# A QKV projection with one level of block products: the first four row tiles loaded ahead of w, w by slices, and two small loads from ScalarE

## The chip, the cores and the metric

The kernel runs on one core of a Trainium2 chip. The metric is the device time of one execution in microseconds (us); lower is better. A profiled execution also has a span, from its first to its last instruction, which is a little shorter than the time.

The core has TensorE (PE in the profile, with its weight loads apart as PEld), VectorE (DVE), ScalarE (ACT), GpSimd (POOL) and SyncE (SP), which here only issues DMA transfers. A "q" behind an engine's name means its instruction queue.

## The reference

```python
def reference(x, w_qkv):              # x 16 x 512 x 768, w_qkv 768 x 2304, float32
    qkv = np.matmul(x, w_qkv)
    q = qkv[..., :768]
    k = qkv[..., 768:1536]
    v = qkv[..., 1536:]
    return np.stack([q, k, v], axis=0).astype(np.float32)
```

So it is one product of an 8192 x 768 matrix with a 768 x 2304 matrix, whose result is written as three matrices of 8192 x 768.

## The kernel before

**Tiling.** The 8192 rows of x are taken as 32 pairs (`p`) of two row tiles (`r`) of 128 rows. The 768 values of K are six slices (`j`, KT = 6) of 128, in two halves of three (KH = 3); partition m of slice j holds row 6 m + j of w. The 2304 columns of w are two groups (`q`) of 1024, each two column blocks (`c`) of CB = 512, and 256 remainder columns between them (`w_rem`, REM).

**Steady state.** From row pair 3 on, each pair and column group is computed with seven block products in place of eight (`product`, lines 238 to 252; `do`, lines 260 to 287). The products need sums and differences of the quarters of w (`sum_w`, lines 119 to 127, VectorE: t1 to t4), of the quarters of x (`sums_x`), and a rounded copy of one quarter of w (`b22`). The remainder columns are plain products (`rem`).

**The start.** Nothing of this can begin before w is there, so the first two row pairs (four row tiles) are computed with plain bf16 products, slice by slice as w lands (`block`, lines 436 to 462): block (q=0, c=0), then (q=0, c=1), then the remainder columns of the two pairs. The same two row pairs meet the second column group later, at lines 571 and 585. Row pair 2 is the first with block products (`u`, line 546 on).

In the start x comes as whole rows (`load_row`), is cast to bf16 (`cast_row`: VectorE one half, ScalarE the other), turned by TensorE against an identity into PSUM and copied out again, half by VectorE and half by ScalarE (`turn_row`). A slice of w is cast by `cast_j`. `busy(n)` issues n matmuls of zeros. `load_x_rows(2)` brings row pair 2 in eight parts, which VectorE transposes (`transpose`) and ScalarE rounds (`round_row`).

**Order.** The schedule is written out by hand: each engine runs its instructions in the order of the program text, and each issuing queue issues its transfers in that order. SP's order at the start is: row tiles 0, 1 and 2 (lines 403 to 407), w's slices 0 to 4 of block c=0 (line 408), row tile 3 (line 409), slice 5 (line 410), block c=1 in two halves (line 411), row pair 2 in eight parts (lines 412 and 418), then the second column group's first block (line 419). GpSimd issues w_rem itself (line 417), after a one-column copy, `mark` (line 414), that waits for the first half of block c=1; later in its order comes the rounding of B22 (line 516).

TensorE's order is lines 489 to 520: 8 fillers, row tile 0 turned, 2 fillers, row tile 1 turned, 1 filler, row tile 2 turned, then the products of block 0 with three row tiles per slice. Row tile 3 is turned between slices 4 and 5, and has its six products behind the others (`three`, line 487).

[...]

Of the kernel before, what the change touches and what calls it, by code (L numbers as in the profile page):

```python
# [10 lines left out]
def kernel(  # L11
# [27 lines left out]
    KT = K // P  # L39
# [3 lines left out]
    CB = 512  # L43
# [23 lines left out]
    xb_pool = ctx.enter_context(tc.tile_pool(name="xb", bufs=4))  # L67
    rem_pool = ctx.enter_context(tc.tile_pool(name="rem", bufs=1))
    s_pool = ctx.enter_context(tc.tile_pool(name="s", bufs=2))
    m_pool = ctx.enter_context(tc.tile_pool(name="m", bufs=1))  # L70
    ps_pool = ctx.enter_context(tc.tile_pool(name="ps", bufs=8, space=bass.MemoryType.PSUM))


# [20 lines left out]

    stage = {}

    def load_first(js):
        if (0, 0, 0) not in stage:
            t = tq_pool.tile([P, KT, CB], fp32, name="st0", tag="tq")
            stage[0, 0, 0], stage[0, 1, 0] = t[:, :KH, :], t[:, KH:, :]  # L100
        for j in js:
            load_w(stage[0, j // KH, 0][:, j % KH:j % KH + 1, :], j, 1, Q_OFF[0], CB)

    def load_blocks(q, c):
        if q == 0:
            t = tq_pool.tile([P, KT, CB], fp32, name="st0", tag="tq")
            for j in range(0, KT, KH):
                load_w(t[:, j:j + KH], j, KH, Q_OFF[q] + c * CB, CB)
            stage[q, 0, c], stage[q, 1, c] = t[:, :KH, :], t[:, KH:, :]
        else:  # L110
            for h in range(2):
                if c == 0 and h == 0:
                    t = st_first
                else:
                    t = st_pool.tile([P, KH, CB], fp32, name="st1", tag="st")[:]
                load_w(t, h * KH, KH, Q_OFF[q] + c * CB, CB)
                stage[q, h, c] = t

    def sum_w(q, n):
        t1, t2, t3, t4 = ts[q]  # L120
# [63 lines left out]
    def turn_row(p, r):  # L184
        if r == 0:
            xb[p] = xb_pool.tile([P, KT, 2 * P], bf16, name="xb", tag="xb")
        cols = xc[p][:, r, :].rearrange("m (p j) -> m j p", j=KT)
        ps = ps_pool.tile([P, KT, P], bf16, name="ps")
        for j in range(KT):
            nc.tensor.transpose(ps[:, j, :], cols[:, j, :], eye)  # L190
        ks = (slice(0, KH), slice(KH, KT))
        copy_halves([xb[p][:, n, r * P:(r + 1) * P] for n in ks], [ps[:, n, :] for n in ks])

    def round_x(p):
        xb[p] = xb_pool.tile([P, KT, 2 * P], bf16, name="xb", tag="xb")
# [205 lines left out]
    zero = xb_pool.tile([P, CB], bf16, name="zero", tag="xb")  # L401
    nc.vector.memset(zero[:], 0.0)
    load_row(0, 0)
    nc.scalar.activation(tiny[:], zero[:, :1], ident)
    make_identity(nc, eye)
    load_row(0, 1)
    load_row(1, 0)
    load_first(range(KT - 1))
    load_row(1, 1)
    load_first((KT - 1, ))  # L410
    load_blocks(0, 1)
    load_x_rows(2, (0, ))
    mark = m_pool.tile([P, 1], fp32, name="mark")
    nc.gpsimd.tensor_copy(out=mark[:], in_=stage[0, 0, 1][:, KH - 1, :1])  # L414
    for h in range(2):
        rows = w_qkv.rearrange("(p j) n -> p j n", j=KT)[:, h * KH:(h + 1) * KH]
        nc.gpsimd.dma_start(w_rem[h][:], rows[:, :, R_OFF:R_OFF + REM])  # L417
    load_x_rows(2, range(1, 8))
    load_blocks(1, 0)

    def busy(n):
# [2 lines left out]
        for _ in range(n):  # L424
            nc.tensor.matmul(ps[:], zero[:, :P], zero[:], start=True, stop=True)

    def cast_j(q, c, w, j, eng=act):
        src = stage[q, j // KH, c][:, j % KH, :]
        if eng is act:
            eng.activation(w[:, j, :], src, ident)  # L430
        else:
            eng.tensor_copy(out=w[:, j, :], in_=src)

    quads = {}

    def block(q, c, w, groups, between={}):

        ps = {}
        late = []

        def finish(n):
            p, r = divmod(n, 2)
            u = quads[p, q]
            act.activation(u.o[:, r, c * CB:(c + 1) * CB], ps[n][:], ident)

        for i, (js, tiles) in enumerate(groups):
            for n in tiles:
                p, r = divmod(n, 2)
                if n not in ps:
                    ps[n] = bank()  # L450
                for j in js:
                    nc.tensor.matmul(  # L452
                        ps[n][:], xb[p][:, j, r * P:(r + 1) * P], w[:, j, :],
                        start=(j == 0), stop=(j == KT - 1), skip_group_check=True,
                    )
# [28 lines left out]
        round_x(p)  # L484
        sums_x(p)

    three = [((j, ), range(3)) for j in range(KT)] + [(range(KT), (3, ))]

    busy(8)
    cast_row(0, 0)  # L490
    turn_row(0, 0)
    busy(2)
    cast_row(0, 1)
    cast_row(1, 0)
    turn_row(0, 1)
    busy(1)
    cast_j(0, 0, b1[0], 0, dve)
    turn_row(1, 0)
    for j in range(1, KT - 1):
        cast_j(0, 0, b1[0], j, dve)  # L500
    cast_row(1, 1)
    cast_j(0, 0, b1[0], KT - 1, dve)
    late0 = block(0, 0, b1[0], three, {KT - 2: lambda: turn_row(1, 1)})
    cast_j(0, 1, bt, 0, dve)
    late0[0]()
    late0[1]()
    cast_j(0, 1, bt, 1, act)
    cast_j(0, 1, bt, 2, dve)
    late0[2]()
    late0[3]()  # L510
    sum_w(0, 1)
    cast_j(0, 1, bt, 3, dve)
    cast_j(0, 1, bt, 4, act)
# [123 lines left out]
```

## Time and profile before

| what | value |
|---|---|
| time, three runs | 361.94, 362.08, 362.61 us; median 362.08 |
| time of the profiled execution | 361.55 us |
| its span | 359.7 us |
| TensorE busy | 351.6 us, 98% |
| VectorE, ScalarE, GpSimd busy | 228.3, 186.4 and 178.8 us |
| mean granted TensorE clock | 0.998 |
| DMA moved | 107.70 MB, 299 GB/s in the mean |

The profile is one execution. Busy time of an engine is the time in which it had an instruction; a busy TensorE may still be waiting inside a row of matmuls, since their ends are modelled. The views used here are the page, the chain of work that ended last in order of time, the instructions of one engine in order of time (start, length, engine, line, operation, what is written from what, count, and in brackets the idle time before it and what ended that), and the busy time of the engines in stretches of one microsecond.

| busy from 0 to 24 us, group | count | mean ns |
|---|---|---|
| matmul of zeros (line 425) | 11 | 609 |
| matmul of a block, 128x512 bf16 (line 452) | 47 | 378 |
| matmul of w_rem, 128x256 bf16 (line 304) | 24 | 272 |
| VectorE cast of a slice of w (line 432) | 9 | 424 to 426 |
| ScalarE cast of half a row tile (line 174) | 4 | 521 |
| VectorE cast, or copy from PSUM, of half a row tile (line 173) | 8 | 358 |
| ScalarE evacuation of a block's tile (line 444) | 8 | 601 |
| GpSimd rounding of B22 (line 516) | 1 | 1717 |

### The profile page before, as it was taken

To read this page: it belongs to the slowest core of one execution; us is meant where nothing else is said; L and a number is where in the kernel's file an instruction comes from. 1 tells how busy PE (TensorE), PEld (TensorE's weight loads), DVE (VectorE), ACT (ScalarE), POOL (GpSimd) and SP (SyncE) were. 2 spreads that over 40 slices of the span, in tenths; PEclk is the share of its full clock that TensorE was granted. 3 is DMA by queue.
4 is the path that set the end of the run, shared out by engine and by line. 5 is a ranking of instruction groups with operands and counts; after the bars stand their busy time and mean duration, and the time that the engine had idled before them with its cause. 6 is when DMAs were issued, how large, how long until landed. Compare 5 with 4: busy or idle time off the path is not lost.

```text
span 359.7 us, 5223 instructions
## 1 busy us (share of the span) xinstructions
PE 351.6 (98%) x1744; PEld 250.9 (70%) x1775; DVE 228.3 (63%) x242; ACT 186.4 (52%) x317; POOL 178.8 (50%) x186
## 2 busy tenths in 40 slices
PE   7999999999999999999999999999999999999995
PEld 3465577777777777777777777777777777777763
DVE  3799676657566675566675556676556676556643
ACT  4569744545444545444455444445545445545452
POOL 0401856436665445665444665444665444666420
PEclk9999999999999999999999999999999999999999
DMA  7999999799999999899999999899999899989766
GB/s 270 351 370 358 334 360 337 224 311 337 276 317 304 291 285 281 289 305 310 294 286 281 290 294 328 282 294 274 295 283 323 295 299 271 296 274 326 285 251 246
DMA packets 81611, 107.70 MB, mean 299 GB/s; under 512 B 5041, under 2 KB 61617, under 8 KB 81585
## 3 DMA queue, kind: packets, MB, share of 16 engines
q1 hardware_dynamic: 66464, 96.35, 82.4%
q10 hardware_dynamic: 14320, 10.62, 8.9%
q0 software_dynamic: 800, 0.39, 0.8%
q8 instruction: 14, 0.23, 0.3%
q14 instruction: 13, 0.10, 0.1%
HBM read 32.24 MB, written 75.50 MB: 300 GB/s over the span
## 4 chain that ended last, share of the span: by engine, by line
PE 92%; DMA 5%; issue 1%; ACT 1%; ACTq 0%; POOL 0%; SPq 0%
PE ps L249 78%; PE ps L304 11%; PE ps L452 3%; DMA st<-in_w_qkv_dram 2%; DMA w_rem<-in_w_qkv_dram 2%; DMA xin<-in_x_dram 1%; ACT o L284 0%; ACTq L359 0%; POOL w_rem L417 0%; SPq L170 0%; ACT orem L373 0%; POOL mark L414 0%; ACTq L375 0%; ACTq L373 0%
## 5 line engine op out<-in xcount | busy, mean ns | idle before, releaser
L249 PE MATMUL ps<-t,s 128*128 128x512 f32 x720 | 181.1, 399 | 0.0
L249 PEld LDWEIGHTS ps<-t,s 128*128 128x128 f32 x720 | 135.0, 188 | 30.7
L196 POOL CAST xb<-xf 128x1536 bf16<-128x1536 f32 x28 | 40.9, 1462 | 132.8 <-DVE xf L161 132.8
L281 DVE TENSOR_TENSOR o<-o,ps 128x512 f32<-128x512 f32 x58 | 39.9, 688 | 90.3 <-ACT o L280 90.3
L161 DVE STREAM_TRANSPOSE xf<-xin 128x1536 f32<-128x1536 f32 (+1 forms) x32 | 88.8, 2779 | 1.6 <-DMA xin<-in_x_dram 1.6
L249 PE MATMUL ps<-b,xb 128*128 128x512 bf16 x331 | 85.1, 380 | 1.5
L249 PEld LDWEIGHTS <-xb 128*128 128x128 bf16 x360 | 32.8, 98 | 37.3 <-issue 7.6
L274 ACT ACTIVATE o<-ps 128x512 f32<-128x512 f32 x60 | 35.9, 598 | 43.7 <-PE ps L249 40.9
L280 ACT ACTIVATE o<-ps 128x512 f32<-128x512 f32 x58 | 34.7, 599 | 44.3 <-PE ps L249 44.3
L287 DVE TENSOR_TENSOR o<-o,ps 128x512 f32<-128x512 f32 x60 | 41.3, 688 | 21.4 <-PE ps L249 20.2
L249 PE MATMUL ps<-b,s 128*128 128x512 f32 x180 | 50.4, 389 | 0.0
L284 ACT ACTIVATE o<-ps 128x512 f32<-128x512 f32 x60 | 35.9, 598 | 24.5 <-PE ps L249 21.6
L258 ACT ACTIVATE o<-ps 128x512 f32<-128x512 f32 x60 | 35.9, 598 | 24.4 <-DVE o L287 20.6
L304 PE MATMUL ps<-w_rem,xb 128*128 128x256 bf16 x384 | 47.5, 273 | 0.3 <-DMA w_rem<-in_w_qkv_dram 0.3
L304 PEld LDWEIGHTS <-xb 128*128 128x128 bf16 x384 | 37.2, 98 | 12.0 <-issue 1.6
L271 DVE TENSOR_TENSOR o<-o,ps 128x512 f32<-128x512 f32 x60 | 37.9, 674 | 2.2 <-ACT o L258 1.6
L249 PEld LDWEIGHTS ps<-b,s 128*128 128x128 f32 x180 | 33.8, 188 | 7.1
L216 POOL TENSOR_TENSOR s<-xf 128x384 fp32r<-128x384 f32 x29 | 30.9, 1065 | 0.0
L217 POOL TENSOR_TENSOR s<-s,xf 128x384 fp32r<-128x384 f32 x29 | 29.5, 1018 | 2.3
L218 POOL TENSOR_TENSOR s<-xf 128x384 fp32r<-128x384 f32 x29 | 29.5, 1017 | 0.0
L220 POOL TENSOR_TENSOR s<-xf,s 128x384 fp32r<-128x384 f32 x29 | 29.5, 1016 | 0.0
L318 ACT ACTIVATE orem<-ps 128x512 f32<-128x512 f32 x31 | 18.5, 596 | 20.1 <-PE ps L304 20.1
(44 smaller groups left out, 119.9 us busy)
## 6 DMA issues: line engine op xcount, KB each, us to landing
out_dram<-o SPq DMA_DIRECT2D x62, 768.0 KB, 5.3
out_dram<-o SPq DMA_DIRECT2D x65, 256.0 KB, 4.2
xin<-in_x_dram SPq DMA_DIRECT2D x62, 192.0 KB, 6.9
xin<-in_x_dram ACTq DMA_DIRECT2D x50, 192.0 KB, 4.6
out_dram<-orem SPq DMA_DIRECT2D x31, 256.0 KB, 5.9
st<-in_w_qkv_dram SPq DMA_DIRECT2D x5, 768.0 KB, 8.7
xin<-in_x_dram SPq DMA_DIRECT2D x4, 384.0 KB, 4.4
st<-in_w_qkv_dram SPq DMA_DIRECT2D x6, 256.0 KB, 5.8
```

The lines of the kernel that those rows point to most:

```text
L161: nc.vector.transpose(turned[:, g:g + n], rows[:, g:g + n])
L196: nc.gpsimd.tensor_copy(out=xb[p][:], in_=xf[p][:])
L216: 1: lambda g: g.tensor_tensor(s[:, 1], a21, a22, op=add),
L249: nc.tensor.matmul(ps[:], lhs[j], rhs[j], start=(start and j == 0), stop=(j == KH - 1), skip_group_check=True,)
L258: nc.scalar.activation(u.o[:, 0, :CB], u.x[:], ident)
L271: nc.vector.tensor_tensor(c11, c11, u.z[:], op=add)
L274: nc.scalar.activation(c12, u.x[:], ident)
L280: nc.scalar.activation(c22, u.x[:], ident)
L281: nc.vector.tensor_tensor(c22, c22, u.y[:], op=add)
L284: nc.scalar.activation(c21, u.x[:], ident)
L287: nc.vector.tensor_tensor(c12, c12, u.y[:], op=add)
L304: nc.tensor.matmul(ps, xb[p][:, j, r * P:(r + 1) * P], w_rem[j // KH][:, j % KH, :], start=(j == 0), stop=(j == KT - 1), skip_group_check= ...
```

## The change

SP's order becomes: row tiles 0, 1, 2 and 3; w's block c=0 by slices, the first slice in two halves of 256 columns; block c=1 by slices, six transfers in place of two; row pair 2 in eight parts with nothing between; then the second column group as before. ScalarE issues two loads first of all, of 32 values (128 bytes) in each of 128 rows: of w's first slice, and of row tile 2 of x. Their destination, `touch`, is read by nothing.

GpSimd's mark now waits for the first slice of block c=1; a second mark, behind w_rem and ahead of B22's rounding, waits for the first half of row pair 2.

`turn_row` puts its two halves into two PSUM tiles and hands back the copies out of PSUM, which the caller issues later. All four row tiles are turned ahead of the first product. Block 0 runs four row tiles per slice; its first slice runs for three of them in two column halves. The first three slices of block c=1 are all cast by VectorE, where ScalarE did the second, and the four evacuations of block 0 are issued behind them.

```diff
-    m_pool = ctx.enter_context(tc.tile_pool(name="m", bufs=1))
+    m_pool = ctx.enter_context(tc.tile_pool(name="m", bufs=2))
...
+    def load_slices(c, cuts):
+        t = tq_pool.tile([P, KT, CB], fp32, name="st0", tag="tq")
+        stage[0, 0, c], stage[0, 1, c] = t[:, :KH, :], t[:, KH:, :]
+        for j, nj, lo, hi in cuts:
+            load_w(t[:, j:j + nj, lo:hi], j, nj, Q_OFF[0] + c * CB + lo, hi - lo)
...
         cols = xc[p][:, r, :].rearrange("m (p j) -> m j p", j=KT)
-        ps = ps_pool.tile([P, KT, P], bf16, name="ps")
+        ks = (slice(0, KH), slice(KH, KT))
+        ps = [ps_pool.tile([P, KH, P], bf16, name="ps") for _ in ks]
         for j in range(KT):
-            nc.tensor.transpose(ps[:, j, :], cols[:, j, :], eye)
-        ks = (slice(0, KH), slice(KH, KT))
-        copy_halves([xb[p][:, n, r * P:(r + 1) * P] for n in ks], [ps[:, n, :] for n in ks])
+            nc.tensor.transpose(ps[j // KH][:, j % KH, :], cols[:, j, :], eye)
+        return lambda: copy_halves(
+            [xb[p][:, n, r * P:(r + 1) * P] for n in ks], [t[:] for t in ps]
+        )
...
     load_row(0, 0)
+    touch = m_pool.tile([P, 2, G], fp32, name="touch")
+    nc.scalar.dma_start(touch[:, 0], w_qkv.rearrange("(p j) n -> p j n", j=KT)[:, 0, :G])
+    nc.scalar.dma_start(touch[:, 1], x_flat[2 * P:3 * P, :G])
     nc.scalar.activation(tiny[:], zero[:, :1], ident)
     make_identity(nc, eye)
     load_row(0, 1)
     load_row(1, 0)
-    load_first(range(KT - 1))
     load_row(1, 1)
-    load_first((KT - 1, ))
-    load_blocks(0, 1)
-    load_x_rows(2, (0, ))
-    mark = m_pool.tile([P, 1], fp32, name="mark")
-    nc.gpsimd.tensor_copy(out=mark[:], in_=stage[0, 0, 1][:, KH - 1, :1])
+    half = CB // 2
+    load_slices(0, [(0, 1, 0, half), (0, 1, half, CB)] + [(j, 1, 0, CB) for j in range(1, KT)])
+    load_slices(1, [(j, 1, 0, CB) for j in range(KT)])
+    load_x_rows(2)
+
+    def hold(src):
+        mark = m_pool.tile([P, 1], fp32, name="mark")
+        nc.gpsimd.tensor_copy(out=mark[:], in_=src)
+
+    hold(stage[0, 0, 1][:, 0, :1])
     for h in range(2):
         rows = w_qkv.rearrange("(p j) n -> p j n", j=KT)[:, h * KH:(h + 1) * KH]
         nc.gpsimd.dma_start(w_rem[h][:], rows[:, :, R_OFF:R_OFF + REM])
-    load_x_rows(2, range(1, 8))
+    hold(xin[2][:, 0, :1])
     load_blocks(1, 0)
...
-    three = [((j, ), range(3)) for j in range(KT)] + [(range(KT), (3, ))]
+    lo, hi = slice(0, half), slice(half, CB)
+    first = [((0, ), range(3), lo), ((0, ), range(3), hi), ((0, ), (3, ))]
+    first += [((j, ), range(4)) for j in range(1, KT)]
 
     busy(8)
     cast_row(0, 0)
-    turn_row(0, 0)
+    turned = [turn_row(0, 0)]
     busy(2)
+    turned[0]()
     cast_row(0, 1)
+    turned.append(turn_row(0, 1))
+    busy(2)
     cast_row(1, 0)
-    turn_row(0, 1)
+    turned[1]()
+    turned.append(turn_row(1, 0))
     busy(1)
-    cast_j(0, 0, b1[0], 0, dve)
-    turn_row(1, 0)
-    for j in range(1, KT - 1):
+    cast_row(1, 1)
+    turned[2]()
+    cast_j(0, 0, b1[0], 0, dve, lo)
+    turned.append(turn_row(1, 1))
+    cast_j(0, 0, b1[0], 0, dve, hi)
+    turned[3]()
+    for j in range(1, KT):
         cast_j(0, 0, b1[0], j, dve)
-    cast_row(1, 1)
-    cast_j(0, 0, b1[0], KT - 1, dve)
-    late0 = block(0, 0, b1[0], three, {KT - 2: lambda: turn_row(1, 1)})
-    cast_j(0, 1, bt, 0, dve)
-    late0[0]()
-    late0[1]()
-    cast_j(0, 1, bt, 1, act)
-    cast_j(0, 1, bt, 2, dve)
-    late0[2]()
-    late0[3]()
+    late0 = block(0, 0, b1[0], first)
+    for j in range(KH):
+        cast_j(0, 1, bt, j, dve)
+    for f in late0:
+        f()
     sum_w(0, 1)
     cast_j(0, 1, bt, 3, dve)
```

`block` and `cast_j` take a range of columns for this. In `block` only the first matmul into a row tile's PSUM bank has the start flag; the second column half and the later slices come without it.

More of the change, by code (lines that the diff above doesn't have):

```diff
@@ L95 @@
     stage = {}
[L97 to L102, printed above, removed]
-    def load_blocks(q, c):
[L105 to L117, printed above, removed]
+    def load_slices(c, cuts):
[3 more added lines that the diff above has]
+            load_w(t[:, j:j + nj, lo:hi], j, nj, Q_OFF[0] + c * CB + lo, hi - lo)
+    def load_blocks(q, c):
+        for h in range(2):
+            if c == 0 and h == 0:
+                t = st_first
+            else:
+                t = st_pool.tile([P, KH, CB], fp32, name="st1", tag="st")[:]
+            load_w(t, h * KH, KH, Q_OFF[q] + c * CB, CB)
+            stage[q, h, c] = t
     def sum_w(q, n):
@@ L425, in busy, with cast_j @@
             nc.tensor.matmul(ps[:], zero[:, :P], zero[:], start=True, stop=True)
-    def cast_j(q, c, w, j, eng=act):
-        src = stage[q, j // KH, c][:, j % KH, :]
+    def cast_j(q, c, w, j, eng=act, n=slice(0, CB)):
+        src = stage[q, j // KH, c][:, j % KH, n]
         if eng is act:
-            eng.activation(w[:, j, :], src, ident)
+            eng.activation(w[:, j, n], src, ident)
         else:
-            eng.tensor_copy(out=w[:, j, :], in_=src)
+            eng.tensor_copy(out=w[:, j, n], in_=src)
     quads = {}
@@ L444, in finish @@
             act.activation(u.o[:, r, c * CB:(c + 1) * CB], ps[n][:], ident)
-        for i, (js, tiles) in enumerate(groups):
+        for i, (js, tiles, *cols) in enumerate(groups):
+            cols = cols[0] if cols else slice(0, CB)
             for n in tiles:
                 p, r = divmod(n, 2)
-                if n not in ps:
+                fresh = n not in ps
+                if fresh:
                     ps[n] = bank()
@@ L452, in block @@
                     nc.tensor.matmul(
-                        ps[n][:], xb[p][:, j, r * P:(r + 1) * P], w[:, j, :],
-                        start=(j == 0), stop=(j == KT - 1), skip_group_check=True,
+                        ps[n][:, cols], xb[p][:, j, r * P:(r + 1) * P], w[:, j, cols],
+                        start=(fresh and j == 0), stop=(j == KT - 1), skip_group_check=True,
                     )
```

## The prediction

> **Order of reading.** First the page: TensorE is busy 98% of the span, and from 22.9 us on the chain of waits lists nothing but matmuls up to the last evacuations at 352 us. So a change to the start is worth just what it takes off, or adds to, the time before that dense stretch, if nothing else in the kernel becomes late. Then the chain in order of time, which says what bounds the start:
>
> ```profile
> 1.65 5.21 DMA xin<-in_x_dram
> 6.88 6.73 DMA st<-in_w_qkv_dram
> 13.67 0.44 POOL mark L414
> 14.11 0.85 POOL w_rem L417
> 14.96 5.42 DMA w_rem<-in_w_qkv_dram
> 20.43 2.45 PE ps L304 x21
> ```
>
> Columns: start, length, what. Until 20.43 us the end is set by loads: rows of x, the first 512 columns of w, the next 512 (c=1), and the remainder columns w_rem, which GpSimd asks for only after the first half of c=1 has landed and its mark is made. Next, TensorE in order of time:
>
> ```profile
> 8.13 3.41 PE L452 MATMUL ps<-b,xb 128*128 128x512 bf16 x15
> 11.67 0.54 PE L190 MATMUL ps<-eye,xc 128*128 128x128 bf16 x6
> 12.20 2.10 PE L452 MATMUL ps<-b,xb 128*128 128x512 bf16 x8
> 14.13 5.65 PE L452 MATMUL ps<-both,xb 128*128 128x512 bf16 x24
> 19.62 0.49 PE L304 MATMUL ps<-w_rem,xb 128*128 128x256 bf16 x3
> 20.43 2.45 PE L304 MATMUL ps<-w_rem,xb 128*128 128x256 bf16 x21 [0.31 <-DMA w_rem<-in_w_qkv_dram]
> ```
>
> The 15 matmuls start every (3.41 - 0.38) / 14 = 0.216 us, those of w_rem every 0.109 us (2.45 less one of 0.27, over 20). Block 0 (24 matmuls; one record is missing) needs 24 x 0.216 = 5.18 us and takes 14.13 - 8.13 = 6.00: 0.82 is the break 11.37 to 12.20, where the fourth row tile is cast, turned and copied. Block 1 needs 5.18 and takes 19.62 - 14.13 = 5.49: 0.31 is lost to the cast of its last slices. Then 3 x 0.109 bring us to 19.95, and TensorE stands still 0.48 us until 20.43. So 1.61 us are there to be won, beside the first matmul's place at 8.13. The landings are read off VectorE, where it waited:
>
> ```profile
> 6.89 0.36 DVE L173 CAST xc<-xin 128x384 bf16<-128x384 f32 x1 [0.80 <-DMA xin<-in_x_dram]
> ...
> 9.47 0.43 DVE L432 CAST b<-st 128x512 bf16<-128x512 f32 x1 [0.22 <-DMA st<-in_w_qkv_dram]
> 10.17 0.43 DVE L432 CAST b<-st 128x512 bf16<-128x512 f32 x1 [0.27 <-DMA st<-in_w_qkv_dram]
> 11.09 0.36 DVE L173 CAST xc<-xin 128x384 bf16<-128x384 f32 x1 [0.50 <-DMA xin<-in_x_dram]
> 11.72 0.43 DVE L432 CAST b<-st 128x512 bf16<-128x512 f32 x1 [0.26 <-DMA st<-in_w_qkv_dram]
> ...
> 16.61 3.02 DVE L127 TENSOR_TENSOR t<-st,t 128x1536 fp32r<-128x1536 f32 x1
> ```
>
> Third row tile 6.89, fourth 11.09, w's sixth slice 11.72: a row tile (384 KB) costs 11.09 - 10.17 = 0.92 us of the queue, a slice (256 KB) about 0.65. Last the stretches of one us (PE, PEld, DVE, ACT, POOL, clock, DMA share, GB/s):
>
> ```profile
> 4.00:5.00 1.00, 1.00 (x6) 0.55 (x5) 0.19 (x1) 0.35 (x1) 0.00 (x0) 1.00 0.88 344
> 5.00:6.00 1.00, 1.00 (x6) 0.37 (x4) 0.54 (x2) 0.15 (x1) 0.00 (x0) 1.00 0.95 282
> 6.00:7.00 1.00, 0.47 (x4) 0.20 (x4) 0.20 (x2) 0.86 (x3) 0.00 (x0) 1.00 1.01 370
> ...
> 11.00:12.00 1.00, 0.87 (x9) 0.38 (x8) 0.64 (x2) 0.52 (x1) 0.00 (x0) 1.00 1.05 410
> ```
>
> The DMA engines are full from 6 us on, but move 344, 282 and 370 GB/s from 4 to 7 us against 410 later: 66 + 128 + 40 = 234 KB are missing, 0.57 us at 410. That is the stretch of the third row tile and of w's first slice, the two places that the new 128-byte loads read ahead.
>
> **Row tile 4 ahead of w.** SP issues its load before w's, so it lands at 6.89 + 0.92 = 7.81 and all of w's slices up to the sixth keep their sum (11.72). TensorE now turns it before the first product: ScalarE's cast 0.52, 0.06 to TensorE, six transposes and a start behind them 0.40, so 7.81 + 0.02 + 0.98 = 8.81. Beside it VectorE casts its half (0.36), copies row tile 3 (0.36) and casts the low half of w's first slice (half of 0.43), each overlapping the next by some 0.08: about 8.80 too. The half slice itself lands at 7.81 + 0.32 = 8.13, earlier than VectorE gets to it. First matmul 8.81 instead of 8.13: **+0.68**. The break goes: **-0.82**. The three further fillers (busy) and the earlier copies lie before 8.13 on idle engines; two PSUM tiles per turn let ScalarE copy beside VectorE, where it waited 3.1 us in all before.
>
> **Column halves and four tiles per slice.** Three matmuls of 512 columns become six of 256: 6 x 0.109 against 3 x 0.216, nothing. Four tiles use 0.86 us per slice and a slice lands every 0.65, so from the second slice (9.10, cast by 9.55, due at 8.81 + 0.86 = 9.67) loads stay ahead. Block 0 ends at 8.81 + 5.18 = 13.99.
>
> **c=1 by slices.** Six issues for two, and two for one in w's first slice: five more at some 0.55 (five took 2.78) are 2.8 us of SP's sequencer. Hidden: SP spends 8.21 to 16.57 on the eight issues for row pair 2, waiting for earlier landings; without that cover row pair 2 would start up to 2.8 us late. The slices land from about 12.4 in steps of 0.65, so VectorE's three casts (now all there) are done by 14.1, sum 1 (1.75) by 15.8, the fourth slice's cast by 16.25; TensorE wants it at 13.99 + 12 x 0.216 = 16.58. ScalarE has four evacuations (2.2) and two casts (1.15) from 13.7: 17.0, wanted at 17.01. So block 1 loses its stall, by a hair: **-0.31**, end 19.17. Bounds: -0.31 and 0.
>
> **w_rem earlier.** The mark now waits for one slice (12.4), not half of c=1 (13.64): GpSimd issues 1.24 us earlier. Low end: w_rem lands at 20.43 - 1.24 = 19.19, wanted at 19.17 + 0.33 = 19.50, the wait is gone, -0.48. High end: the DMA engines are full anyway, w_rem shares them with row pair 2 and lands at 20.43 as before; then everything won so far is waited away here. From 17 to 18 us 314 of 391 packets were w_rem's: once its descriptors are there it goes ahead of row pair 2. So nearer the low end; I take a landing at 19.60, a wait of 0.10: **-0.38**.
> [...]
>
> **Rounding B22 later** takes GpSimd's 1.7 us off VectorE's sum 2, which took 3.02 beside it against 1.75 alone. No time on the path: TensorE needs B22 only after 27.4 us, and it is made by about 20.5. It now runs beside the transposes of row pair 2, where no row shows the pair: 0 to 1.27 us. The cover: row pair 2's first half is wanted at about 22.0, and transposed (1.54) and rounded (0.85) by 20.5, or 21.8. The second mark queues only B22 behind it.
>
> **The two small loads.** ScalarE issues them before its table load (0.73 to 2.0) and is wanted at 3.83; at 0.43 each they hide. On the engines 256 packets: upper bound from w_rem's 512-byte packets, 117.2% of 16 engine-us for 314, 60 ns, so 256 x 60 / 16 = 0.96 us; lower bound a gain of 0.57, if the missing 234 KB come back. Both shift all loads, hence everything above. A quarter of 512 bytes is nearer the low price; I take 0.3 spent, 0.3 won: **0**.
> [...]
>
> **Sum.** 0.68 - 0.82 - 0.31 - 0.38 = -0.83 us. Later work keeps it: row pair 2's sums had about 1.2 us to spare before TensorE's use at 25.24, the next slices' casts about 1.0. The profiled execution took 361.55 (span 359.7, 1.85 around it), the runs 362.08 in the median, 0.53 more; -0.83 on the median is 361.25, I say **361.2**.
>
> **Rivals.**
> 1. *The wait moves to w_rem* (0.22). For it: full DMA engines from 6 to 20 us, and the same bytes. Against: the 314 packets. TensorE is held to about 20.43 and the gain is 0 to 0.2: 361.9 to 362.1. The case that the small loads warm nothing and cost 0.6 to 0.8 ends here too.
> 2. *The small loads pay in full* (0.20). For it: 282 GB/s exactly where w's first slice begins. Then loads come 0.57 earlier: -1.4, 360.7.
> 3. *The small loads sit ahead of the first row tile on the same engines* (0.13): they queue with it from 1.7 us, it lands at up to 4.8, and the chain of rows keeps the 0.96. From 0.83 on the change loses. At the full price with w_rem held as well: first matmul 9.77, block 1 ends 20.13, w_rem 20.43 + 0.96 = 21.39: +0.96, 363.0. Against: early engines are not full (267 GB/s from 2 to 3 us), so part hides.
>
> The forecast itself has 0.45. Its own range is 360.9 to 361.6. What can be told from no change is 0.2%, 0.72 us, so faster means below 361.36: two thirds of the forecast (0.30), rival 2 (0.20), a little of rival 1: 0.52. Same: the rest of the forecast and most of rival 1: 0.34. Slower: rival 3 and a remainder: 0.14. The range 360.3 to 362.6 leaves out the far ends of rivals 2 and 3.
>
> **What would show it.** First product near 8.8 with no break up to 19.2; row tile 4's cast near 7.8; the mark near 12.4; the w_rem wait at 0.1 or gone; sum 2 at 1.75; GB/s from 4 to 7 us near 400 for rival 2. I am wrong if the first row tile's cast moves from 3.83 by more than 0.5, if the w_rem wait is 0.5 or more, or if a new wait stands between 22 and 46 us.

## The result, and the profile after

| what | before | after |
|---|---|---|
| time, median of 22 runs each | 362.06 us (361.37 to 363.53) | 361.15 us (360.58 to 362.73) |
| ratio after / before | | 0.9979, 95% interval 0.9970 to 0.9988 |
| time of the profiled execution | 361.55 us | 360.69 us |
| its span | 359.7 us | 358.9 us |
| mean granted TensorE clock | 0.998 | 1.0 |

The change takes 0.91 us off in the median, about 0.2%. The prediction said 361.2 with a range of 360.3 to 362.6. Its sum was -0.83; in the two profiled executions it is made up of other terms than were forecast, as the views show.

First the start of the chain of waits of the changed kernel (start, length, what):

```profile
2.12 5.36 DMA xin<-in_x_dram
7.50 4.54 DMA st<-in_w_qkv_dram
13.38 6.39 DMA w_rem<-in_w_qkv_dram
19.82 2.45 PE ps L299 x21
```

The same four loads bound the start as before. TensorE is released for good at 19.82 instead of 20.43, 0.61 earlier, and w_rem's transfer now takes 6.39 us from issue to landing, where it took 5.42. TensorE in order of time:

```profile
8.08 0.54 PE L184 MATMUL ps<-eye,xc 128*128 128x128 bf16 x6 [0.34 <-ACT xc L167]
8.45 5.38 PE L456 MATMUL ps<-b,xb 128*128 128x256 bf16 x27
13.67 5.34 PE L456 MATMUL ps<-both,xb 128*128 128x512 bf16 x24
18.85 0.49 PE L299 MATMUL ps<-w_rem,xb 128*128 128x256 bf16 x3
19.82 2.45 PE L299 MATMUL ps<-w_rem,xb 128*128 128x256 bf16 x21 [0.48 <-DMA w_rem<-in_w_qkv_dram]
```

The break at 11.67 is gone: block 0 takes 13.67 - 8.45 = 5.22 us, block 1 takes 18.85 - 13.67 = 5.18. Both are dense. The three matmuls of w_rem end at 18.85 + 3 x 0.109 = 19.18, and TensorE stands still until 19.82: **0.64 us**, more than the 0.48 of before. From there the two executions run in step, up to the last row of w_rem's matmuls (the first line is from before, the second from after):

```profile
354.86 0.83 PE L304 MATMUL ps<-w_rem,xb 128*128 128x256 bf16 x6
354.27 0.83 PE L299 MATMUL ps<-w_rem,xb 128*128 128x256 bf16 x6
```

That is 0.59 earlier, but the time of the profiled execution is 0.86 less. The time less the start of this row was 6.69 us and is 6.42: 0.27 us lie behind the last matmuls. They aren't in the transfers of the last outputs, which are 0.6 earlier too (the DMA engines fall idle between 357.4 and 357.6, where it was between 358.0 and 358.2). No term of the prediction is about this end.

VectorE in order of time, for the landings and what lies next to the rounding of B22:

```profile
4.11 0.36 DVE L166 CAST xc<-xin 128x384 bf16<-128x384 f32 x1 [2.98 <-DMA xin<-in_x_dram]
...
6.35 0.36 DVE L166 CAST xc<-xin 128x384 bf16<-128x384 f32 x1 [0.63 <-DMA xin<-in_x_dram]
...
7.50 0.36 DVE L166 CAST xc<-xin 128x384 bf16<-128x384 f32 x1 [0.52 <-DMA xin<-in_x_dram]
...
15.74 1.75 DVE L120 TENSOR_TENSOR t<-st,t 128x1536 fp32r<-128x1536 f32 x1
17.58 1.60 DVE L154 STREAM_TRANSPOSE xf<-xin 128x768 f32<-128x768 f32 x1
20.85 1.57 DVE L154 STREAM_TRANSPOSE xf<-xin 128x768 f32<-128x768 f32 x1 [1.67 <-DMA xin<-in_x_dram]
```

The first row tile lands 0.28 later than before (4.11 against 3.83), the third 0.54 earlier (6.35 against 6.89), the fourth at 7.50. Sum 2 is back at 1.75 us. GpSimd:

```profile
12.09 0.44 POOL L414 COPY mark<-st 128x1 f32<-128x1 f32 x1 [10.78 <-DMA st<-in_w_qkv_dram]
12.47 1.70 POOL L419 DMA_DIRECT2D w_rem<-in_w_qkv_dram  x2
...
17.74 1.47 POOL L525 CAST b<-st 128x1536 fp32r<-128x1536 f32 x1
```

The mark is made 1.58 us earlier than before (13.67), yet w_rem lands only 0.61 earlier. B22's rounding now lies beside the transpose at 17.58, which takes 1.60; the other transpose, with no work of GpSimd beside it, takes 1.57. The stretches of one us (PE, PEld, DVE, ACT, POOL, clock, DMA share, GB/s):

```profile
4.00:5.00 1.00, 0.76 (x7) 0.32 (x6) 0.36 (x1) 0.52 (x1) 0.00 (x0) 1.00 0.99 363
5.00:6.00 1.00, 0.66 (x6) 0.16 (x4) 0.62 (x2) 0.74 (x2) 0.00 (x0) 1.00 1.00 350
6.00:7.00 1.00, 0.78 (x8) 0.56 (x9) 0.64 (x2) 0.81 (x3) 0.00 (x0) 1.00 0.99 360
```

The stretch that moved 344, 282 and 370 GB/s now moves 363, 350 and 360: 77 KB of the 234 KB that were missing are back.

### The profile page after: what moved, and what is told of

The parts are those of the page before. It is cut to its first block, busy times and chain, and to the rows that moved or that the text cites. A ratio compares the mean times of both kernels' runs of the same rounds, so it can differ in the third digit from the quotient of the medians.

```text
span 358.9 us, 5279 instructions
## 1 busy us (share of the span) xinstructions
PE 352.3 (98%) x1780; PEld 251.0 (70%) x1780; DVE 227.4 (63%) x244; ACT 185.7 (52%) x316; POOL 178.6 (50%) x187
## 4 chain that ended last, share of the span: by engine, by line
PE 92%; DMA 5%; ACT 1%; ACTq 0%; POOL 0%; SPq 0%; issue 0%
PE ps L244 78%; PE ps L299 11%; PE ps L456 3%; DMA w_rem<-in_w_qkv_dram 2%; DMA xin<-in_x_dram 1%; DMA st<-in_w_qkv_dram 1%; SPq L163 0%; ACT o L279 0%; ACTq L354 0%; POOL w_rem L419 0%; ACT orem L368 0%; POOL mark L414 0%; ACTq L370 0%; ACTq L368 0%
## 5 line engine op out<-in xcount | busy, mean ns | idle before, releaser
L244 PE MATMUL ps<-b,xb 128*128 128x512 bf16 x360 | 87.7, 380 | 0.0
L213 POOL TENSOR_TENSOR s<-xf 128x384 fp32r<-128x384 f32 x29 | 29.4, 1013 | 0.0
L211 POOL TENSOR_TENSOR s<-xf 128x384 fp32r<-128x384 f32 x29 | 29.3, 1011 | 0.0
```

The source lines that it names most:

```text
L244: nc.tensor.matmul(ps[:], lhs[j], rhs[j], start=(start and j == 0), stop=(j == KH - 1), skip_group_check=True,)
```

## The experiments

All kernels compute the whole result. Each time is a median beside runs of the kernel before on the same chip: 362.18 us (29 runs) for e1 to e4, 362.15 (29) for e5, e6, e8 and e10, 361.89 (35) for e7, e11, e12 and e13. The ratios come with the comparison and need not be the quotients of these medians. A profile is one execution and carries the spread of one: e13 is the changed kernel once more, and its profiled execution takes 361.47, its median 360.94.

Times of the start in all profiles. "Row 4" is VectorE's cast of the fourth row tile (its landing), "mark" GpSimd's first mark, "go" the start of w_rem's second half on TensorE, "end" the start of the last row of w_rem's matmuls, and "time - end" the time of the profiled execution less that. (In e6 VectorE had other work ahead of row 4's cast, so 9.20 is no landing there.)

| kernel | first row | row 4 | first product | mark - row 4 | go - row 4 | end | time - end | ratio to before, 95% |
|---|---|---|---|---|---|---|---|---|
| before | 3.83 | 11.09 | 8.13 | | | 354.86 | 6.69 | |
| after | 4.11 | 7.50 | 8.45 | 4.59 | 12.32 | 354.27 | 6.42 | 0.9979, 0.9970 to 0.9988 |
| e13 after again | 4.01 | 7.88 | 8.84 | 4.60 | 12.73 | 355.06 | 6.41 | 0.9978, 0.9968 to 0.9988 |
| e1 no small loads | 3.72 | 8.21 | 9.16 | 4.59 | 13.01 | 355.65 | 6.55 | 0.9982, 0.9970 to 0.9994 |
| e2 small loads alone | 4.12 | 10.86 | 8.11 | | | 354.77 | 6.79 | 0.9991, 0.9976 to 1.0005 |
| e3 w_rem late | 4.10 | 8.91 | 9.86 | 6.16 | 12.84 | 356.20 | 6.43 | 0.9983, 0.9968 to 0.9998 |
| e4 w_rem early | 4.09 | 8.05 | 9.01 | 3.30 | 12.41 | 354.91 | 6.42 | 0.9961, 0.9946 to 0.9976 |
| e5 B22 early | 4.13 | 7.84 | 8.79 | 4.59 | 12.59 | 354.87 | 6.42 | 0.9977, 0.9964 to 0.9990 |
| e7 c=1 in halves | 4.03 | 7.75 | 8.70 | 5.88 | 12.46 | 354.66 | 7.03 | 1.0014, 0.9998 to 1.0030 |
| e8 row pair 2 held | 3.86 | 7.56 | 8.61 | 4.61 | no wait | 354.25 | 6.46 | 0.9974, 0.9959 to 0.9990 |
| e10 w_rem from SP | 3.80 | 7.90 | 8.85 | | no wait | 355.45 | 6.53 | 0.9990, 0.9975 to 1.0004 |
| e11 row 4 turned ahead | 3.91 | 7.89 | 9.00 | | no wait | 355.43 | 6.99 | 1.0016, 1.0003 to 1.0029 |
| e12 order | 3.86 | 8.28 | 9.23 | | no wait | 354.74 | 6.42 | 0.9974, 0.9964 to 0.9985 |
| e6 row 4 alone | 3.62 | 9.20 | 11.59 | | no wait | 358.47 | 6.69 | 1.0093, 1.0059 to 1.0126 |

The column "time - end" parts the kernels in two: 6.41 to 6.55 where block c=1 comes by slices, 6.69 to 7.03 where it comes in halves (before, e2, e6, e7, e11). This is not only the spread of single profiles. The part of it that lies outside the span is on record for every run: 1.74 to 1.86 us in the 12 of e13 (median 1.77), 1.77 to 2.07 in the 35 of the kernel before beside them (median 1.97). So 0.2 us of e13's gain lie outside the span. The profiles show as much again inside it, behind the last matmuls: from the start of their last row to the end of the span it is 4.8 us before, 4.6 after and in e13. The cause of both is open.

**The small loads (e1, e2).** e1 is the changed kernel without them, e2 the kernel before with nothing but them (and its second buffer).

```diff
-    touch = m_pool.tile([P, 2, G], fp32, name="touch")
-    nc.scalar.dma_start(touch[:, 0], w_qkv.rearrange("(p j) n -> p j n", j=KT)[:, 0, :G])
-    nc.scalar.dma_start(touch[:, 1], x_flat[2 * P:3 * P, :G])
```

> The changed kernel without ScalarE's two 128-byte loads. Theory A, the loads cost and win about as much (0.21 us of the engines by 256 packets of 13 ns, against the cold start of w's first slice): first product within 0.2 us of the 8.45 of the changed kernel, last row of w_rem within 0.2 of 354.27, time as the changed kernel's 361.2. Rival B, they pay in full: the loads of the third and fourth row tile land 0.3 to 0.6 us later (the fourth at 7.8 to 8.1 in place of 7.50), first product 8.8 to 9.0, GB/s from 5 to 6 us back near 280, time 361.5 to 361.8. Rival C, they are pure cost: the first row tile lands at 3.8 in place of 4.11 and all is 0.2 to 0.3 earlier.

> The kernel before with ScalarE's two small loads alone. Theory A: third row tile's cast within 0.3 us of 6.89, end within 0.2 of before, 362.1. Rival B, they pay in full: third row tile 6.3, w's slices 0.5 earlier, and since w_rem follows its mark the end comes 0.5 earlier, 361.6. Rival C: first row tile 4.1 and everything 0.2 to 0.3 later, 362.3.

Measured: 361.72 without them (12 runs), 361.84 with them alone (12 runs). Over all profiles of the study the first row tile is cast at 3.62 to 3.91 in the four without them (mean 3.77) and at 3.80 to 4.13 in the ten with them (mean 4.01): they cost 0.24 us there. The third row tile is cast at 6.36 to 7.77 without (mean 7.07) and at 6.1 to 7.98 with them (mean 6.72): 0.35 earlier, with a spread five times as large, so a gain there isn't shown. What they take of the engines is small. The queue of ScalarE's loads in the changed kernel from 3 to 4 us (packets, MB, share of the 16 engines):

```profile
q10 hardware_dynamic: 121, 0.01, 9.4%
```

By this 9.4% of 16 engine-us over 121 packets, an estimate is 12 ns each. The times lean to a gain, 0.34 us in the medians of e2 (361.84 against 362.18) and, by the ratios of after and e1 (0.9979 and 0.9982), 0.1; neither interval parts it from nothing. No harm from them can be seen; whether they gain anything stays open.

**w_rem's mark moved both ways (e3, e4).** e3 waits with the mark for the third slice of c=1, about where it stood before; e4 for the fifth slice of c=0.

```diff
-    hold(stage[0, 0, 1][:, 0, :1])
+    hold(stage[0, 0, 1][:, KH - 1, :1])      # e3
+    hold(stage[0, 1, 0][:, 1, :1])           # e4
```

> The changed kernel with the mark on the third slice of block c=1, as before, in place of the first: GpSimd asks for w_rem 1.3 us later. Theory A, w_rem goes as soon as it is asked for: it lands near 21.1 in place of 19.82, TensorE waits 1.9 us in place of 0.65, last row of w_rem 355.5 in place of 354.27, time 362.4, that is slower than the kernel before. Rival B, the full engines set the landing whatever the mark does: landing 19.8 to 20.4, time 361.2 to 361.8.

> The changed kernel with the mark on the fifth slice of block c=0: GpSimd asks for w_rem 1.2 us earlier. Theory A: w_rem lands near 18.6, the wait of 0.65 us is gone, last row of w_rem 353.7 in place of 354.27, time 360.6, unless block c=1 is late (its fourth to sixth slices share the engines with w_rem then and may land up to 1 us later, a stall of up to 0.5). Rival B, full engines: w_rem lands at 19.5 or later and the time stays 361.1.

Measured: 361.48 (12 runs) and 361.16 (6 runs). The late mark was to cost all that was won, and did not. The table says why: counted from the fourth row tile, the mark moves over 2.86 us (3.30 to 6.16), and w_rem's go over 0.43 (12.41 to 12.84), while two profiles of one and the same kernel differ by 0.41 (12.32 and 12.73). When w_rem lands hardly depends on when it is asked for: its second half takes 5.34 us from issue to landing in e3, 6.39 and 6.79 in the two profiles of the changed kernel, 7.76 in e4. A small gain from asking early isn't excluded: e4 has the lowest ratio of all, 0.9961, from six runs, though its block 1 takes 5.39 us, and VectorE's sum 2 waits 0.52 us for the last slices of c=1, as it would if they now share the engines with w_rem. In the changed kernel GpSimd asks, from 12.47 on, while the engines are full of c=1 (a DMA share of 1.04 to 1.05 from 12 to 15 us), and then w_rem shares them with row pair 2. The DMA queues from 17 to 18 us (packets, MB, share of the 16 engines), first two lines of before, then two of the changed kernel:

```profile
q0 software_dynamic: 314, 0.16, 117.2%
q1 hardware_dynamic: 77, 0.05, 21.5%
...
q0 software_dynamic: 280, 0.14, 102.2%
q1 hardware_dynamic: 127, 0.09, 32.7%
```

The queue of GpSimd's w_rem moved 280 packets beside 127 of SP's row pair 2. Before, it was 314 beside 77. I had taken the 314 as a sign that w_rem goes ahead of the rest; in the changed kernel's stretch it goes about two packets to one. So neither queue was simply first in that stretch; what decides between them, no run here shows.

**Row pair 2 out of w_rem's way (e8).** If the sharing sets w_rem, then holding back row pair 2 must free it. e8 keeps SP from issuing the second half of row pair 2 until c=1's last slice is there (a small GpSimd copy into `xin` comes ahead of it).

```diff
-    load_x_rows(2)
+    load_x_rows(2, range(4))
...
+    nc.gpsimd.tensor_copy(out=xin[2][:, 4:, 0], in_=stage[0, 1, 1][:, KH - 1, :4])
+    load_x_rows(2, range(4, 8))
```

> The changed kernel with row pair 2's second half (parts 5 to 8) held back on SP until block c=1 has wholly landed, so that fewer of its packets share the engines with w_rem. Theory C, w_rem's landing is set by what shares the DMA engines with it: w_rem lands 0.3 to 0.6 us earlier than in the changed kernel by the same landing of row tile 3, TensorE's wait falls from 0.65 to 0.1 to 0.4, time 360.7 to 361.0. Rival: w_rem's landing does not move, since its own 768 packets set it, time 361.1 to 361.3; or row pair 2 comes late and TensorE waits behind w_rem's rows.

Measured: 361.32 (12 runs), 0.9974, no other than the changed kernel. TensorE and VectorE in its profile, each in order of time:

```profile
18.98 2.78 PE L299 MATMUL ps<-w_rem,xb 128*128 128x256 bf16 x24
21.59 1.46 PE L244 MATMUL ps<-b,xb 128*128 128x512 bf16 x5
22.89 1.55 PE L299 MATMUL ps<-w_rem,xb 128*128 128x256 bf16 x12
24.58 0.73 PE L244 MATMUL ps<-t,s 128*128 128x512 f32 x2
```

```profile
21.10 1.58 DVE L154 STREAM_TRANSPOSE xf<-xin 128x768 f32<-128x768 f32 x1 [1.85 <-DMA xin<-in_x_dram]
```

All 24 matmuls of w_rem run in one piece: the wait is gone, and w_rem's halves take 5.2 and 5.6 us from issue to landing, where it was 5.9 and 6.4 (asked for from 12.55 on, the second is in use at 19.31, 18.98 + 3 x 0.109, where it was 19.82). So the sharing was its cause. But row pair 2's second half is there at 21.10 instead of 20.85, and behind its transpose, ScalarE's rounding (22.72) and an evacuation (23.94) TensorE now stops for 0.4 us ahead of 24.58. The wait has moved to the next load in the same row.

**Other ways past it (e10, e12).** e10 loads w_rem on SP's queue as float32, ahead of row pair 2, and GpSimd casts it (the first mark is left out). e12 is e8 with the hold one slice earlier, and with row pair 2's first product and its evacuation ahead of ScalarE's second rounding.

```diff
+    for h in range(2):                                                     # e10
+        load_w(wst[:, h * KH:(h + 1) * KH], h * KH, KH, R_OFF, REM)
...
-        nc.gpsimd.dma_start(w_rem[h][:], rows[:, :, R_OFF:R_OFF + REM])
+        nc.gpsimd.tensor_copy(out=w_rem[h][:], in_=wst[:, h * KH:(h + 1) * KH])
```

```diff
+    nc.gpsimd.tensor_copy(out=xin[2][:, 4:, 0], in_=stage[0, 1, 1][:, KH - 2, :4])     # e12
+    load_x_rows(2, range(4, 8))
...
+    u = quad(2, 0)
+    do(u, 1)
```

> The changed kernel with w_rem loaded by SP as float32, in its order behind block c=1 and ahead of row pair 2, and cast by GpSimd (two casts of 0.73 us). Theory C: nothing shares the engines with it, it lands at about 16.5 and 17.5, is cast by 18.3, and TensorE's wait is gone: last row of w_rem 353.6 to 353.7 in place of 354.27, time 360.4 to 360.7. Row pair 2 lands at about 20.7 as now. Rival: the wait is not DMA sharing, and a wait of like size comes up next (row pair 2's transposes and copies behind w_rem's rows), time 361.0 or more.

> An attempt to beat the changed kernel: row pair 2's second half held back until the fifth slice of c=1 has landed (so w_rem shares the engines with less), and TensorE's first product of row pair 2 with its evacuation put ahead of ScalarE's second rounding of row pair 2. Theory C: the wait for w_rem is at most 0.3 and the next wait (0.4 in the run with the half held to the sixth slice) at most 0.2; last w_rem row less first product 345.2 to 345.5 in place of 345.82, time 360.7 to 361.0. Rival: the DMA engines' total up to row pair 2 sets it, and what w_rem gains is waited away at row pair 2: difference 345.6 or more, time as the changed kernel.

Measured: e10 361.88 (12 runs), a miss: w_rem's wait is gone, but row pair 2 is transposed at 19.77 and 22.32, and TensorE waits 0.28 and 0.39 for it. e12 361.10 (12 runs) beside 360.94 (12 runs) for e13, the changed kernel, on the same chip: no difference that can be told.

> The changed kernel once more, to be compared on this chip with the three others of this call and for a second profile of its start: time 360.9 to 361.4; first product 0.98 us behind row tile 3's landing, whatever the landing is in this execution; a wait for w_rem of 0.5 to 1.0.

Measured: 360.94 (12 runs). TensorE in its profile, in order of time:

```profile
8.84 5.38 PE L456 MATMUL ps<-b,xb 128*128 128x256 bf16 x26
14.05 5.34 PE L456 MATMUL ps<-both,xb 128*128 128x512 bf16 x24
19.23 0.49 PE L299 MATMUL ps<-w_rem,xb 128*128 128x256 bf16 x3
20.61 2.45 PE L299 MATMUL ps<-w_rem,xb 128*128 128x256 bf16 x21 [0.89 <-DMA w_rem<-in_w_qkv_dram]
```

The first product is 0.96 behind the fourth row tile, and the wait for w_rem is 20.61 - (19.23 + 0.33) = 1.05, just above what was expected. Here TensorE is released 0.18 later than in the profile of before, though the median is 0.95 less than before's. The two don't contradict each other: e13's profiled execution (361.47) is among the slowest of its 12 runs, those of before (361.55) and after (360.69) are each faster than all but one of the 22 runs. Two profiles show how the parts of one start hang together. They don't show what each part is worth of the 0.9 us in the medians.

Three kernels (e8, e10, e12) rid TensorE of the wait for w_rem and none is faster than the changed kernel by more than can be told. I take what is left of the start to be the sum of the bytes up to row pair 2, through engines that are full (a DMA share of 0.99 or more in every us from 3 to 20 in the changed kernel); no run moves fewer bytes, so that is argued, not shown.

**The fourth row tile alone (e6).** The kernel before with its SP order changed and the fourth tile turned ahead, but with the old `turn_row`, whose copies follow at once and share one PSUM tile.

```diff
-    load_first(range(KT - 1))
     load_row(1, 1)
-    load_first((KT - 1, ))
+    load_first(range(KT))
...
-    three = [((j, ), range(3)) for j in range(KT)] + [(range(KT), (3, ))]
+    three = [((j, ), range(4)) for j in range(KT)]
...
+    turn_row(1, 1)
+    for j in range(KT):
+        cast_j(0, 0, b1[0], j, dve)
+    late0 = block(0, 0, b1[0], three)
```

> The kernel before with one part of the change: row tile 3 loaded ahead of w and turned ahead of the first product, four row tiles per slice; w's first slice whole, the turn with one PSUM tile, c=1 in halves, mark and B22 as before, no small loads. Theory A (first product 0.98 us behind the landing of row tile 3, plus 0.3 to 0.6 for the turn's two copies in a row and the whole slice): first product 9.2 to 9.6, no break, block 0 ends at 14.4 to 14.8 in place of 14.13, and TensorE waits for w_rem until 20.4 as before: time 362.1, no change, since w_rem's landing is what the start waits for. Rival: the break taken away is the gain, time 361.4 or less.

Measured: 366.11 (6 runs, 362.46 to 366.94), the largest miss of the study. ScalarE, then TensorE, in order of time, and the stretches of one us:

```profile
8.43 0.49 ACT L174 ACTIVATE xb<-ps 128x384 bf16<-128x384 bf16 x1
9.31 0.49 ACT L174 ACTIVATE xb<-ps 128x384 bf16<-128x384 bf16 x1 [0.40 <-DVE xb L173]
9.70 0.51 ACT L174 ACTIVATE xc<-xin 128x384 bf16<-128x384 f32 x1
```

```profile
8.35 0.54 PE L190 MATMUL ps<-eye,xc 128*128 128x128 bf16 x6 [1.29 <-ACT xc L174]
10.27 0.54 PE L190 MATMUL ps<-eye,xc 128*128 128x128 bf16 x6 [1.39 <-ACT xc L174]
11.59 6.75 PE L451 MATMUL ps<-b,xb 128*128 128x512 bf16 x23 [0.78 <-DVE b L431]
```

```profile
11.00:12.00 1.00, 0.41 (x2) 0.13 (x2) 1.00 (x4) 0.49 (x1) 0.00 (x0) 0.53 1.05 408
12.00:13.00 1.00, 1.00 (x4) 0.43 (x3) 1.00 (x4) 0.00 (x0) 0.00 (x0) 0.50 1.04 404
13.00:14.00 1.00, 1.00 (x4) 0.30 (x2) 0.21 (x1) 0.00 (x0) 0.00 (x0) 0.50 1.06 412
14.00:15.00 1.00, 1.00 (x5) 0.40 (x4) 0.48 (x2) 0.00 (x0) 0.45 (x2) 0.76 1.05 393
```

Two things go wrong at once. ScalarE's cast of the fourth tile stands behind its copies, and the copy at 9.31 waits for VectorE, which copies from the same PSUM tile. So the cast runs at 9.70, though VectorE had its half at 9.20, and the first product is at 11.59. And TensorE, idle for 1.29, 1.39 and 0.78 us between its groups, is granted half its clock from 11.07 to 14.48 (0.53 in the first stretch is 0.07 us at full and 0.93 at half; 0.76 in the last is 0.48 at half): 3.41 us, of which 2.89 lie under the products and cost, as an estimate, half of that, 1.45: this row of 23 takes 6.75, and e11's row of 23 takes 5.35, in an execution with a mean clock of 0.998. Most of the loss goes with the clock: of the six runs, the one with a mean clock of 0.998 took 362.46, the five with 0.990 to 0.994 took 365.16 to 366.94. The deferred copies and the two PSUM tiles, and the fillers between the turns, are together part of what the move of the fourth tile needs; no run parts one from the other. (0.9 of the delay is this profile's own: its third row tile is cast at 7.77.)

**The fourth row tile with the new turning (e11).** The changed kernel without the small loads, with w's first slice whole, c=1 in halves, the mark on the first half, and no hold on B22's rounding.

```diff
-    load_slices(0, [(0, 1, 0, half), (0, 1, half, CB)] + [(j, 1, 0, CB) for j in range(1, KT)])
-    load_slices(1, [(j, 1, 0, CB) for j in range(KT)])
+    load_slices(0, [(j, 1, 0, CB) for j in range(KT)])
+    load_slices(1, [(j, KH, 0, CB) for j in range(0, KT, KH)])
...
-    hold(stage[0, 0, 1][:, 0, :1])
+    hold(stage[0, 0, 1][:, KH - 1, :1])
...
-    hold(xin[2][:, 0, :1])
```

> Row tile 3 ahead of w with the change's turning (copies handed back and issued later, two PSUM tiles, its fillers) and four row tiles per slice; w's first slice whole, c=1 in halves, mark and B22 as before, no small loads. It is told apart from the run of row tile 3 alone, which came out 4 us slower. Theory D, that run lost 1.5 us to the half clock (3.41 us granted at 0.5) and the rest to ScalarE's order, where the cast of row tile 3 stood behind both copies of row tile 2; so here the first product is 1.1 to 1.3 us behind row tile 3's landing, the clock stays full, and the time is between the two kernels, 361.6 to 362.1. Rival, loading row tile 3 ahead is the loss itself: first product 10 or later, a stretch at half clock, 363 or more.

Measured: 362.45 (12 runs), slower than before by 0.16%. The first product is at 9.00 and the clock stays full under block 0, as expected: its row of 23 takes 5.35 us, where e6's takes 6.75. But block 1 stalls. The instructions of all engines in order of time, from 15 to 19 us:

```profile
16.15 1.58 POOL L519 CAST b<-st 128x1536 fp32r<-128x1536 f32 x1 [0.38 <-DMA st<-in_w_qkv_dram]
16.32 1.69 DVE L430 CAST both<-st 128x512 bf16<-128x512 f32 x1
...
18.07 1.24 PE L452 MATMUL ps<-both,xb 128*128 128x512 bf16 x5 [1.12 <-DVE both L430]
```

VectorE's cast of the fourth slice takes 1.69 instead of 0.43, since GpSimd began to round B22 0.17 us ahead of it. TensorE waits 1.12 us for it.

**c=1 by slices, and B22's hold, one at a time (e7, e5).** e7 is the changed kernel with c=1 in halves and the mark on the first one; e5 is it without the second hold.

```diff
-    load_slices(1, [(j, 1, 0, CB) for j in range(KT)])
+    load_slices(1, [(j, KH, 0, CB) for j in range(0, KT, KH)])      # e7
...
-    hold(xin[2][:, 0, :1])                                          # e5
```

> The changed kernel with block c=1 in two transfers of three slices, as before, and so the mark on the whole first half. By the start of the last w_rem row less the start of the first product (346.73 before, 345.82 in the changed kernel): theory C, w_rem's landing bounds the start and follows its mark by about half; block 1 gets its stall of 0.3 back, but that lies inside the wait for w_rem: difference 346.1 to 346.4, time 361.3 to 361.7. Rival, each part adds its own: 0.3 for the stall and 1.3 for the mark, difference 347 or more, time 362.4.

> The changed kernel without the second mark, so that GpSimd rounds B22 as soon as block c=1 has landed, as before. Theory A, rounding later is off the path: sum 2 takes about 3.0 us in place of 1.75 and the first transpose of row pair 2 begins near 18.9 in place of 17.58, but TensorE needs row pair 2 only at about 22, so its wait stays w_rem's and the time is the changed kernel's within 0.2%. Rival: row pair 2 becomes late, a new wait of TensorE behind w_rem's rows of 0.3 us or more, and the time 361.5 or more.

Measured: e7 361.97 (12 runs) beside 360.94 for e13: 1.03 us, all of the gain. e5 361.37 (12 runs), no difference that can be told from the changed kernel. Of e7's 1.03 us, 0.62 lie behind the last matmuls of the two profiles (7.03 against 6.41 in the table). Of these, 0.35 lie outside the span, and all runs bear them out: e7's time exceeds its span by 2.09 to 2.20 us (12 runs, median 2.12), e13's by 1.74 to 1.86. What in the halves makes the end longer, no view shows. At the start, e7's profile has VectorE and then TensorE in order of time:

```profile
13.60 1.10 DVE L434 CAST both<-st 128x512 bf16<-128x512 f32 x3 [1.47 <-DMA st<-in_w_qkv_dram]
...
16.28 0.42 DVE L434 CAST both<-st 128x512 bf16<-128x512 f32 x1
```

```profile
8.70 5.39 PE L456 MATMUL ps<-b,xb 128*128 128x256 bf16 x26
14.07 5.42 PE L456 MATMUL ps<-both,xb 128*128 128x512 bf16 x24
```

The first slice of c=1 can be cast only when its whole half is there, so TensorE stands for 14.07 - (8.70 + 5.18) = 0.19 us ahead of block 1. The fourth slice is cast from 16.28 to 16.70 and TensorE loads its next weights at 16.75: the cast is on the edge, and block 1 takes 5.27. But this start is not later than e13's (end 354.66 against 355.06), in an execution that is among the fastest of e7's runs. That the fourth slice's cast is over the edge in others is argued, not shown.

In e5, B22's rounding meets sum 2 (GpSimd, then VectorE, in order of time):

```profile
16.51 3.05 POOL L524 CAST b<-st 128x1536 fp32r<-128x1536 f32 x1 [2.01 <-DMA st<-in_w_qkv_dram]
```

```profile
16.47 1.76 DVE L120 TENSOR_TENSOR t<-st,t 128x1536 fp32r<-128x1536 f32 x1 [0.32 <-DMA st<-in_w_qkv_dram]
```

This time VectorE began 0.04 us earlier and it is GpSimd that pays, and nobody waits for B22 yet. In the kernel before, GpSimd was first, and sum 2 paid (3.02 us from 16.61):

```profile
16.30 1.72 POOL L516 CAST b<-st 128x1536 fp32r<-128x1536 f32 x1 [0.56 <-DMA st<-in_w_qkv_dram]
```

## Why the prediction came out right, and where its terms were wrong

The way was right and the size was (-0.83 forecast, -0.91 in the medians, -0.86 between the two profiled executions), but between these two executions errors of opposite sign cancel in it, and a part of the gain lies where no term was. By the profiles before and after, with e13's, the changed kernel once more, beside them:

| step | forecast | after | e13 |
|---|---|---|---|
| first product | +0.68 | +0.32 (8.45 - 8.13) | +0.71 (8.84 - 8.13) |
| break in block 0 | -0.82 | -0.78 (5.22 - 6.00) | -0.79 (5.21 - 6.00) |
| stall in block 1 | -0.31 | -0.31 (5.18 - 5.49) | -0.31 (5.18 - 5.49) |
| wait for w_rem | -0.38 | +0.16 (0.64 - 0.48) | +0.57 (1.05 - 0.48) |
| sum | -0.83 | -0.61 | +0.18 |
| behind the last matmuls | none | -0.27 (6.42 - 6.69) | -0.28 (6.41 - 6.69) |

The break, the stall and the end come out alike in both profiles. The first product and the wait for w_rem move with the landings of one execution, and in both the wait grew where it was to shrink. So the mechanism of three of the terms was right, that of the fourth was not, and that the size came out is in part luck: between before and after, an early first product (0.36 better than forecast) and the end of the kernel (0.27) make up for the wait for w_rem (0.54 worse).

**The fourth row tile's path.** The step "7.81 + 0.02 + 0.98" was right in its second half: the first product is 0.95 or 0.96 behind VectorE's cast of the tile in nine of the eleven profiles that turn it the changed way (7.50 and 8.45; 8.21 and 9.16; 8.91 and 9.86), 1.05 in e8 and 1.11 in e11. The landing in the profiled execution was 0.31 earlier than forecast, and that is luck, not a fault of the 7.81. It is not a constant: over these eleven profiles it lies between 7.50 and 8.91, with a median of 7.89, and the 7.50 of the profiled execution is the earliest of all.

**The small loads** at 0 were taken as 0.3 spent and 0.3 won. Spent were 0.24 at the first row tile, which has cover, because the fourth tile and not the first sets the first product; the third came 0.35 earlier, which its spread doesn't let one call won. So nothing speaks against the 0. Rival 3 named the right place, but its price is a quarter of the 0.96: the packets were bounded at 60 ns each, and take 12 by the estimate above. Rival 2 was to show near 400 GB/s from 4 to 7 us; it is 350 to 363.

**The wait for w_rem** is the step that failed: "w_rem earlier", -0.38, by a landing of 19.60 near the low end ("once its descriptors are there it goes ahead of row pair 2"). It landed at 19.82 though the loads ahead of it were 0.3 earlier than forecast, and the wait grew, to 0.64 (1.05 in e13). My own bound for being wrong, a wait of 0.5 or more, was met. e3 and e4 show that the time of the request counts for little, e8 that the sharing with row pair 2 makes the wait: rival 1's mechanism was right. Its end, TensorE held to about 20.43, was missed only in the one profile: there w_rem landed 0.61 earlier, of which some 0.27 belong to all loads ahead of it (w's sixth slice is cast at 11.45 instead of 11.72). In e13, e4 and e5 TensorE is released at 20.61, 20.46 and 20.43. The gain in the medians is above the 0 to 0.2 of that rival all the same. What went wrong in the working: the 314 packets were read as precedence, in a stretch where row pair 2's requests were only starting to come.

**c=1 by slices** at -0.31 was right in both profiles of the changed kernel, and called "by a hair". In e1 and e3, whose third row tile is late (7.26 and 7.98), the hair is not there: block 1 takes 5.85 and 5.75 us, waiting for ScalarE's cast of a late slice of c=1. TensorE in e1:

```profile
14.35 3.19 PE L453 MATMUL ps<-both,xb 128*128 128x512 bf16 x14
18.05 2.32 PE L453 MATMUL ps<-both,xb 128*128 128x512 bf16 x10 [0.51 <-ACT both L429]
```

What I did not see is how much else hangs on the slices: with halves (e7) the whole gain is gone in the medians, over half of it behind the last matmuls. The forecast took the 1.85 us around the span as fixed; they are not.

**B22 later** was costed as no time on the path, with sum 2 as the only thing beside it. That holds when c=1 comes by slices (e5). With halves the cast of the fourth slice is beside it, and then it is worth up to 1.12 us (e11). The transposes were given 0 to 1.27; they lose nothing that can be seen (1.60 beside B22, 1.57 alone).

**"Busy on idle engines"**, the further fillers, early copies and two PSUM tiles that I costed at nothing, are no ornament: without them (e6) the order on ScalarE and, by the clocks of its runs above all, the halved clock make the kernel 4 us slower than before in the medians (366.11 against 362.15).

That no new wait stands between 22 and 46 us was right, with one addition: row pair 2 has only some 0.3 us in hand (an estimate: the evacuation that e8 waits for ends at 24.28 in the changed kernel, its next product starts at 24.63), which e8, e10 and e12 used up.

## What to carry to other kernels

When the DMA engines are full, an earlier request need not bring an earlier landing (by e3 and e4 the mark moved over 2.86 us and w_rem's go over 0.43): ask what shares the engines with it, and look for the next load in the row before moving one out of the way. A gain at the start counts as far as the last wait before the dense stretch lets it through, so follow it to there and take the sum at that point; then look at the end of the kernel as well, which can change with it (here by 0.27 us). When an early step is moved, move with it the copies that stand in its engine queues and the fillers between TensorE's groups, or the move can cost more than the break it removes: e6, with the old copies and fillers, was granted half the clock for 3.41 us and took 366.11, e11, with the new ones, ran block 0 at the full rate and took 362.45.

## What the hardware showed that was not expected

- **In four overlaps VectorE and GpSimd ran nearly one behind the other, and the later one paid.** Before, B22's rounding began at 16.30 and ended at 18.02; sum 2, begun at 16.61, ended 1.61 us behind that, nearly the whole 1.75 that it takes alone. In e11 the cast begun 0.17 behind B22 ended 0.28 behind it. In e5 sum 2 began first, and B22 ended 1.33 behind it. In e10 two casts of w_rem (an estimate of 0.73 each alone, half of B22's 1.47 for twice the columns), begun beside sum 2, ended 1.45 behind it. Not every pair does so: the transpose takes 1.60 beside B22 and 1.57 alone. What sets the two kinds of pair apart, no run here shows.
- **A few of a load's 16 reports can be late at the start** and shift the whole execution. In the traces of before and after, the casts that waited for a row tile begin 0.02 to 0.03 us behind the last of its 16 reports (3.81 and 3.83, 6.87 and 6.89 before; 4.08 and 4.11, 7.48 and 7.50 after). Before, 14 of the third row tile's are in by 5.76 us, and the last two come at 6.53 and 6.87. In e3 15 of the 16 reports of the third row tile are in by 6.41 us and the last at 7.96 (cast at 7.98), and one report stays over 1 us behind for the next eight loads. In e1 four of them come at 7.14 to 7.24 (cast at 7.26), where the middle ones come at 5.7 to 5.8; its profiled execution takes 362.2 us, its median is 361.72. Between the two profiles of the changed kernel itself w_rem's go differs by 0.79 (19.82 and 20.61), so differences of half a us between single profiles of the start say nothing.
- **Half the clock for 3.41 us** came in e6 (0.50 from 12 to 14 us) without one long gap: in the 3.41 us before it, from 7.66 to 11.07, TensorE had two groups of six transposes (0.54 us each) and nothing else, and never stood for longer than 1.39 us in one piece. A gap of that length alone did not bring it: TensorE stood for 1.38 us in e3, whose mean clock is 1.0. What brings it, no run here shows.
